# Rotary embedding on one core: VectorE and GpSimd start at slot 120 of 128

## The chip, the core and the metric

The kernel runs on one core of a Trainium2 chip. A core has several engines with an instruction list of its own each: TensorE (PE in the profile) for matrix products, VectorE (DVE) and GpSimd (POOL) for elementwise work, ScalarE (ACT) for functions and copies, SyncE (SP), which here only issues transfers. Sixteen DMA engines move data between the main memory (HBM) and the on-chip memory; a transfer is issued by an instruction of SP or of ACT and joins that engine's queue. Engines wait for one another and for transfers by semaphores. The metric is the device time of one execution in microseconds (us); less is better.

## The reference

For x of shape (8, 2048, 8, 64) and tables cos and sin of shape (2048, 32), all float32:

```python
x1 = x[..., : x.shape[-1] // 2]
x2 = x[..., x.shape[-1] // 2 :]
out1 = x1 * cos - x2 * sin     # cos, sin broadcast over batch and head
out2 = x1 * sin + x2 * cos
return np.concatenate([out1, out2], axis=-1)
```

So each element is read once, multiplied by a cosine, and gets its partner from the other half times a sine added. x and the result have 33.55 MB each.

## The kernel before

**Tiling.** The 2048 positions of one batch are laid over the 128 partitions, 16 to each; a batch is then one tile `xt` of 128x8192 float32 (4 MB). There are five such buffers (NBUF = 5). Batches 0 to 4 are loaded at the start, and the load of batch b + 5 is issued behind the work on batch b; it needs the buffer, and so waits until the store of batch b is done. Loads go to SP's queue; stores of batches 0 to 6 go to ACT's queue, those of the last batch to SP's. The result overwrites `xt` before it is stored. Batch 0 is loaded in three parts and stored in two, batch 7 is stored in three.

**Work on a batch.** `rotate` treats a piece of 128x2048 (the two halves of a quarter in batches 0 and 7 are 128x1024). A piece has one of three kinds:

- kind A (29 pieces): POOL makes `t2`, the partner times the sine, in two products (line 122); DVE makes `t1`, x times the cosine (line 129), and adds the two into `xt` (line 136);
- kind B (the first piece of batches 2, 4 and 5): the same two products, but TensorE adds them by multiplying with a unit matrix `eye` (lines 143 and 144), and ACT copies the sum back (line 145);
- kind C (the first piece of batches 1 and 3): DVE makes both products (lines 129 and 148), TensorE adds them with `eye` or its negative `neye` (lines 160 and 161), and ACT copies the sum back (line 165).

**The start.** ACT issues the load of sin (line 76), SP those of the first quarter of batch 0, of cos, and of the rest (lines 67 and 69). POOL writes `eye` by a memset and a select (lines 80 and 81). When sin has landed, ACT writes `nsin`, `sin_ps` and `neye` (lines 90 to 92). When cos has landed, DVE copies it to `cos_ps` (line 93). Then the loop over batches begins.

**Order.** Nearly every instruction stands in `keep(...)`, which holds it at its place in the written order; the order of an engine's instructions is that of the program text. What an engine does first on the page is its part of a barrier of all engines (line 208 in the profile), and last its part of a closing barrier (line 219). Beside the instructions of the program text the lists hold small ones: where an instruction waits for more semaphores than fit into it, an EVENT_SEMAPHORE instruction ahead of it waits for the rest.

Of the kernel before, what the change touches and what calls it, by code (L numbers as in the profile page):

```python
# [10 lines left out]
def kernel(  # L11
# [7 lines left out]
    nc = tc.nc  # L19
    keep = tc.keep_in_program_order  # L20
# [30 lines left out]
    eye = const_pool.tile([P, P], f32, tag="eye")  # L51
# [25 lines left out]
    for b in range(NBUF):  # L77
        load(b)

    nc.gpsimd.memset(eye, 0.0)  # L80
    nc.gpsimd.affine_select(
        out=eye,
        in_=eye,
# [140 lines left out]
```

## Time and profile before

| | |
|---|---|
| time, median of 3 runs | 163.61 us (163.48 to 163.63) |
| span of the profiled execution | 161.8 us, 459 instructions |
| around the span (median less span) | 1.8 us |
| DVE busy | 140.1 us (87%), 66 instructions |
| POOL busy | 138.9 us (86%), 70 instructions |
| PE busy | 49.4 us, ACT 12.8 us |
| moved by DMA | 67.65 MB, 418 GB/s over the span |

The profile is of one execution; its own time is given only as the span, from the first to the last of the program's instructions. The median is that of other, timed runs; it is 1.8 us above the span, for what lies ahead of and behind the program. Busy time is the time in which an engine worked; waits, branches and the issue of transfers are not in it. A share of the whole span says little of a single stage: DVE, for one, stands still for the first 6.93 us and is nearly always busy from there to the last add.

The queues in the DMA part of the page are q1 (SP's), q10 (ACT's) and one called "instruction", over which the engines' instruction lists are brought in.

### The profile page before, as it was taken

Reading aid. Unit: us, or ns where it says so; the run is one execution under the profiler, and the core shown is the slowest. Engines: PE = TensorE matmul, PEld = TensorE weight load, DVE = VectorE, ACT = ScalarE, POOL = GpSimd, SP = SyncE. Lnnn points to the kernel's source line nnn. Section 1 sums busy time; section 2 is a strip of 40 time slices with the busy share of each in tenths; the row PEclk is TensorE's granted clock in tenths of the full one; section 3 lists DMA queues with packets and bytes.
Section 4 is the critical chain, followed back from the end, with each engine's and each line's share of the span. In section 5 each row is a group of like instructions: output and inputs, shape, how many; then the busy total and the mean of one; then the engine's idle time right before and its main releaser. Section 6 shows DMA issues by size and latency. Waiting matters only on the chain.

```text
span 161.8 us, 459 instructions
## 1 busy us (share of the span) xinstructions
PE 49.4 (31%) x80; PEld 18.5 (11%) x80; DVE 140.1 (87%) x66; ACT 12.8 (8%) x14; POOL 138.9 (86%) x70
## 2 busy tenths in 40 slices
PE   0000000597309760978049714972000000000000
PEld 0000000142004220322023301330000000000000
DVE  0297999999999999999999999199989999899950
ACT  3300000002200220021000220022000000000000
POOL 1399997998999999992999959999899997999800
PEclk9999999999975998589957995699655555555555
DMA  5999999999999999899899999999999999999995
GB/s 158 425 454 494 413 308 446 413 470 405 462 405 462 389 502 405 389 510 397 389 510 397 389 512 397 397 502 397 397 488 413 405 478 413 405 478 409 397 419 225
DMA packets 3314, 67.65 MB, mean 418 GB/s; under 512 B 368, under 2 KB 368, under 8 KB 624
## 3 DMA queue, kind: packets, MB, share of 16 engines
q1 hardware_dynamic: 2016, 38.01, 55.5%
q10 hardware_dynamic: 1296, 29.62, 42.6%
q14 instruction: 2, 0.02, 0.0%
HBM read 34.08 MB, written 33.55 MB: 418 GB/s over the span
## 4 chain that ended last, share of the span: by engine, by line
DMA 48%; DVE 37%; POOL 9%; issue 2%; DVEq 0%; SPq 0%; POOLq 0%; ACTq 0%
DMA xt<-in_x_dram 26%; DVE t L129 18%; DMA out_dram<-xt 18%; DVE xt L136 17%; POOL t L122 9%; DMA sin_sb<-in_sin_dram 4%; DVE t L148 1%; DVEq L136 0%; SPq L67 0%; POOLq L122 0%; ACTq L74 0%
## 5 line engine op out<-in xcount | busy, mean ns | idle before, releaser
L122 POOL TENSOR_TENSOR t<-xt,sin_sb 128x1024 f32<-128x1024 f32 (+1 forms) x32 | 70.4, 2199 | 13.5 <-DMA xt<-in_x_dram 8.3
L129 DVE TENSOR_TENSOR t<-xt,cos_ps 128x2048 f32<-128x2048 f32 (+1 forms) x34 | 73.4, 2167 | 0.8
L122 POOL TENSOR_TENSOR t<-xt,nsin 128x1024 f32<-128x1024 f32 (+1 forms) x32 | 70.3, 2196 | 0.0
L136 DVE TENSOR_TENSOR xt<-t,t 128x2048 f32<-128x2048 f32 (+1 forms) x29 | 62.2, 2145 | 8.2 <-POOL t L122 5.5
L143 PE MATMUL o<-t,eye 128*128 128x512 f32 x24 | 17.0, 799 | 23.1 <-DVE t L129 19.6
L160 PE MATMUL o<-t,eye 128*128 128x512 f32 x16 | 12.0, 844 | 37.8 <-DVE t L129 35.6
L144 PE MATMUL o<-t,eye 128*128 128x512 f32 x24 | 14.9, 709 | 0.0
L145 ACT COPY xt<-o 128x1024 f32<-128x1024 f32 x6 | 6.1, 1012 | 45.7 <-PE o L144 45.7
L143 PEld LDWEIGHTS o<-t,eye 128*128 128x128 f32 x24 | 5.5, 256 | 32.5 <-issue 26.5
L160 PEld LDWEIGHTS o<-t,eye 128*128 128x128 f32 x16 | 3.7, 256 | 43.2 <-issue 39.4
L165 ACT COPY xt<-o 128x1024 f32<-128x1024 f32 x4 | 4.0, 1012 | 47.8 <-PE o L161 47.8
L93 DVE COPY cos_ps<-cos_sb 128x512 f32<-128x512 f32 x1 | 0.7, 695 | 6.9 <-DMA cos_sb<-in_cos_dram 6.9
L144 PEld LDWEIGHTS o<-t,eye 128*128 128x128 f32 x24 | 5.6, 234 | 8.2 <-issue 7.6
L161 PE MATMUL o<-t,neye 128*128 128x512 f32 x8 | 6.3, 875 | 0.2
L148 DVE TENSOR_TENSOR t<-xt,sin_ps 128x2048 f32<-128x2048 f32 x2 | 4.6, 2281 | 0.0
L161 PE MATMUL o<-t,eye 128*128 128x512 f32 x8 | 4.1, 592 | 0.0
L161 PEld LDWEIGHTS o<-t,neye 128*128 128x128 f32 x8 | 2.2, 300 | 5.3 <-issue 3.6
L161 PEld LDWEIGHTS o<-t,eye 128*128 128x128 f32 x8 | 1.5, 190 | 1.9 <-issue 1.9
L90 ACT ACT_TABLE_LOAD x1 | 1.3, 1283 | 1.2 <-PEq L208 1.2
L90 ACT ACTIVATE nsin<-sin_sb 128x512 f32<-128x512 f32 x1 | 0.6, 629 | 4.0 <-DMA sin_sb<-in_sin_dram 4.0
L91 ACT COPY sin_ps<-sin_sb 128x512 f32<-128x512 f32 x1 | 0.6, 580 | 0.0
L80 POOL MEMSET eye<- 128x128 f32 x1 | 0.2, 204 | 0.3 <-POOLq L208 0.3
(6 smaller groups left out, 1.0 us busy)
## 6 DMA issues: line engine op xcount, KB each, us to landing
xt<-in_x_dram SPq DMA_DIRECT2D x7, 4096.0 KB, 42.8
out_dram<-xt ACTq DMA_DIRECT2D x6, 4096.0 KB, 27.2
out_dram<-xt ACTq DMA_DIRECT2D x2, 2048.0 KB, 22.3
xt<-in_x_dram SPq DMA_DIRECT2D x2, 1024.0 KB, 6.7
xt<-in_x_dram SPq DMA_DIRECT2D x1, 2048.0 KB, 12.2
out_dram<-xt SPq DMA_DIRECT2D x1, 2048.0 KB, 9.9
out_dram<-xt SPq DMA_DIRECT2D x2, 1024.0 KB, 6.2
sin_sb<-in_sin_dram ACTq DMA_DIRECT2D x1, 256.0 KB, 5.7
```

Of the source, the lines that this page charges most:

```text
L90: keep(nc.scalar.mul(nsin, sin_sb, -1.0))
L93: keep(nc.vector.tensor_copy(cos_ps, cos_sb))
L122: nc.gpsimd.tensor_mul(out=t2u[:, :, u, :].rearrange("p (r h) d -> p r h d", h=H), in0=xu[:, :, 1 - u, :].rearrange("p (r h) d -> p r h d" ...
L129: nc.vector.tensor_mul(out=t1.rearrange("p (r k d) -> p r k d", r=nr, d=Dh), in0=xk, in1=rep(cos_ps[:, r0 : r0 + nr, :], 2 * H),)
L136: keep(nc.vector.tensor_add(out=xt, in0=t1, in1=t2))
L143: nc.tensor.matmul(oc, eye, t1[:, cs], start=True, stop=False)
L144: nc.tensor.matmul(oc, eye, t2[:, cs], start=False, stop=True)
L145: keep(nc.scalar.copy(xt[:, 2 * j * C : 2 * (j + 1) * C], o))
L148: nc.vector.tensor_mul(out=t2.rearrange("p (r k d) -> p r k d", r=nr, d=Dh), in0=xk, in1=rep(sin_ps[:, r0 : r0 + nr, :], 2 * H),)
L160: nc.tensor.matmul(oc, eye, t1u[:, gs, u, :], start=True, stop=False)
L161: nc.tensor.matmul(oc, eye if u else neye, t2u[:, gs, 1 - u, :], start=False, stop=True)
L165: nc.scalar.copy(xu[:, :, u, :], o.rearrange("p (g d) -> p g d", d=Dh))
```

## The change

Two directives are put ahead of POOL's first instruction of the program text and ahead of DVE's, and the memset behind them is held in its place:

```diff
-    nc.gpsimd.memset(eye, 0.0)
+    for eng in (nc.vector, nc.gpsimd):
+        keep(eng.addr_align(128, offset=120))
+    keep(nc.gpsimd.memset(eye, 0.0))
     nc.gpsimd.affine_select(
```

`addr_align(128, offset=120)` is not an instruction that the engine runs. When the program is loaded it is dropped, and empty instructions are put in its place, as many as it takes for the instruction behind it to stand 120 slots past a multiple of 128 in that engine's list (a slot is the place of one instruction). That can be none and at most 127, and the engine runs through all of them. On DVE the instruction behind it is the copy to `cos_ps`, on POOL the first one of writing `eye`. Both directives stand behind the opening barrier. No other instruction is added, taken out or moved on any engine; line numbers behind the change grow by two.

## The prediction
> **What bounds the kernel now.** I began with the page's slices of the span.
>
> ```profile
> DVE  0297999999999999999999999199989999899950
> POOL 1399997998999999992999959999899997999800
> DMA  5999999999999999899899999999999999999995
> DMA packets 3314, 67.65 MB, mean 418 GB/s; under 512 B 368, under 2 KB 368, under 8 KB 624
> ```
>
> Each digit is 4.05 us. The DMA engines are full from the second slice to the last but one; DVE and POOL are nearly full too, but each has its empty part at the left edge. What ended the empty parts is in the waits of the two engines, of which I read POOL's and then DVE's:
>
> ```profile
> POOL t L122 <- DMA xt<-in_x_dram: 8.3, 6, 3.0
> POOL t L122 <- DMA sin_sb<-in_sin_dram: 5.2, 1, 5.2
> ...
> DVE cos_ps L93 <- DMA cos_sb<-in_cos_dram: 6.9, 1, 6.9
> DVE xt L136 <- POOL t L122: 5.5, 4, 3.6
> ```
>
> (total us, times, longest). At the start both wait for tables. Later POOL waits six times for a batch to land, 8.3 us in all, and DVE four times for POOL. The timeline of the first 8 us puts places to this:
>
> ```profile
> 0.73 0.20 POOL L80 MEMSET eye<- 128x128 f32 x1 [0.29 <-POOLq L208]
> ...
> 1.01 0.29 POOL L81 TENSOR_SCALAR_AFFINE_SELECT eye<-eye 128x128 f32<-128x128 f32 x1
> ...
> 6.53 1.26 POOL L122 TENSOR_TENSOR t<-xt,sin_sb 128x512 f32<-128x512 f32 x1 [5.23 <-DMA sin_sb<-in_sin_dram]
> 6.93 0.69 DVE L93 COPY cos_ps<-cos_sb 128x512 f32<-128x512 f32 x1 [6.93 <-DMA cos_sb<-in_cos_dram]
> ...
> 7.53 0.30 ACT L92 ACTIVATE neye<-eye 128x128 f32<-128x128 f32 x1
> ```
>
> The chain that ended last, in order of time, holds these two pieces:
>
> ```profile
> 62.55 28.82 DMA out_dram<-xt
> ...
> 91.50 42.82 DMA xt<-in_x_dram
> ```
>
> The store of batch 2 frees a buffer, the load of batch 7 takes it, lands at 134.3, and the last 21.6 us of compute and the last store follow. But the load waited in its queue: batch 6, ahead of it, landed only at 114.9 (POOL's wait for it ends there), 23 us after batch 7's load was issued. Both queues together were moving all that the DMA engines could. So the bound is the DMA, with a tail of compute behind the last load; DVE and POOL come close behind.
>
> **The change, part by part.** *The empty instructions, their number.* The program's lists show one directive on each of the two engines, no count. It depends on the slot at which each list stood before, which no view shows. The page has two packets on the instruction queue within the span,
>
> ```profile
> q14 instruction: 2, 0.02, 0.0%
> ```
>
> and the trace's packet records put them at 94.4 and 120.0 us, 8192 bytes and 309 ns each. I read each as an engine that enters a new block of its list and has a further block brought in, and 8192 bytes as 128 slots (64 bytes each). At 94.4 DVE's sequencer stood at its 65th entry (waits counted), at 120.0 POOL's stood at about its 70th to 74th. If the packets are theirs, a block ended there, DVE's copy (third entry) stood at slot 66 and POOL's memset at some 62 to 66, and the padding is 54 to 58 on both. That the two agree speaks for it; but TensorE and ScalarE were also moving near 94, so I keep 0 and 127 as ends and take 55.
>
> *Price of one.* No row has an empty instruction. The nearest are entries that the sequencer deals with alone: two MODIFY_POOL_CONFIG of POOL start 30 ns apart (0.88 and 0.91), two semaphore waits of POOL 78 ns (0.53 and 0.61), two of DVE 69 ns (119.24 and 119.31), all met at once. So 30 to 78 ns on POOL and 30 to 69 ns on DVE; as the semaphore entries do more than an empty one, I take 50 ns. That makes 55 x 0.05 = 2.75 us on each (the ends: 0, and 127 x 0.078 = 9.9 us on POOL, 127 x 0.069 = 8.8 us on DVE).
>
> [...]
>
> *What covers it.* POOL is done with the opening barrier at 0.73, needs 0.57 us for `eye` (0.73 to 1.30), and has nothing to do until the first quarter of batch 0 (6.30) and sin (6.46) are there: 6.30 - 0.73 - 0.57 = 5.0 us of cover. DVE waits from 0.69 to 6.93: 6.2 us. With 2.75 us both are covered, cost 0. `eye` is ready at 1.30 + 2.75 = 4.05; ScalarE takes it at 7.53, TensorE at 30.1: cost 0. SP and ACT issue all the first loads by themselves and wait for neither engine: cost 0. If the cover is gone, POOL is late by up to 9.9 - 5.0 = 4.9 us and DVE by up to 8.8 - 6.2 = 2.6. The delay runs on into the chain, and the stores of batches 0 to 2 are late by as much. It would not reach the end, though: POOL waits for the landings of batches 1, 2 and 4 for 0.9, 0.7 and 3.0 us and for batch 5's for 1.7, which swallows 6.3 us by 96 us; while stores are missing, the loads have the DMA engines to themselves and land rather sooner; and the load of batch 7 has 23 us in its queue. From 134.45 on nothing is left to swallow a delay.
>
> *The block's end, moved.* With the first instruction at slot 120 a block ends 8 slots on: on DVE behind the add at 11.63, on POOL at about 10 us. Before, DVE's adds and products around 94.4 follow each other at the usual 2.40 us (92.47 to 94.86), POOL's around 120.0 at 2.28 (119.59 to 121.86): entering a block cost nothing measurable. I take 0 here as well; the packet itself is 0.3 us of one of 16 engines. The upper end, if the block were not there in time: what a fresh transfer needs in that crowd, 6.7 us for a 1 MB load of batch 0. It would fall on both engines at once, at a place from where the later waits swallow most.
>
> [...]
>
> *`keep` on the memset.* The lists show the same order as before: 0.
>
> **Sum.** 161.8 us of span + 0 + 0 + 0, and 1.8 us around it: 163.6, the median of the runs (163.61).
>
> **Rivals.**
> *Slower, a long padding* (0.12). Padding near 127 at near 78 ns, from the point where it passes 5.0 us on POOL. Against it: 54 to 58 by the packets, and the waits that swallow. If the early delay is paid in full in the chain (store of batch 2, load of batch 7), it costs up to 4.9; with half of that, 163.6 + 2.4 = 166.0.
> *Slower, a block's end in a bad place* (0.18). DVE's 111 entries from the copy on now end at slot 231, before at 177; the next block's end, at 256, is 25 slots into what follows instead of 79. If the closing part is longer than 25 and the block isn't there, or if the block at 10 us isn't, the stall decides. For it: the closing part lies behind everything and hides nothing. Against it: blocks were there in time twice before. Price: 0.3 us (a packet) to 6.7; near the low end, since a block has over 140 us to come: 163.6 + 1.0 = 164.6.
> *Faster, later stores* (0.16). If the padding is visible by 1 to 3 us, loads land sooner for want of stores beside them, and the waits for batches 1 to 7 shrink. The last, 1.14 us at 134.45 for batch 7, is the gain if it goes whole: 162.5. The DMA share of the last 5.8 us is only 0.67, so there is room. Against it: with 55 x 0.05 nothing is visible. A share of it comes at 0.4 to 0.6 us.
> *Nothing happens* (padding of few or no instructions) ends at 163.6 like the forecast and is in its chance.
>
> **Numbers.** The measurement tells about 0.2% from no change, 0.33 us. Forecast, hidden padding (or none): 0.54, within 0.2%. Faster 0.16, slower 0.12 + 0.18 = 0.30. The likeliest case alone has 163.3 to 163.9. For 8 in 10 I leave out the better half of the faster case (0.08) and most of the long padding (0.10), which gives 163.0 to 165.2.
>
> **What would show it.** Right: DVE's copy still starts at about 6.93, POOL's first product at 6.53, `eye` at 2 to 5 us instead of 0.73, and batch 7's product still at 134.45. The two packets of the instruction queue move to about 10 to 13 us. Wrong: POOL's first product later than 6.6 (padding not covered); a gap of over 0.2 us in DVE or POOL between 9 and 13 us with no semaphore behind it (block not there); the span unchanged but the time not (closing part); a shorter or longer wait for batch 7.

## The result, and the profile after

The changed kernel takes 164.29 us (median of 5 runs, 163.99 to 164.47) against 163.60 us (163.48 to 163.63): ratio 1.0037, 95% interval 1.0026 to 1.0048. A second comparison of the same two kernels gave 163.98 against 163.59 us, ratio 1.0020 (1.0011 to 1.0029). The change costs 0.2 to 0.4%. Both times lie inside the stated range; the first is clear of the forecast "within 0.2%", the second at its edge. The span of the profiled execution grew from 161.8 to 162.5 us. Every ratio here leaves out slow executions, those over 1.5% above the fastest of their kernel: five of the eleven of `branch_8` and one each of `wait_only` and `copy_1`.

The start went as forecast. From the timeline of the changed kernel (start, us, engine, line, operation, tiles; line numbers are two higher):

```profile
2.81 0.20 POOL L82 MEMSET eye<- 128x128 f32 x1 [2.37 <-issue]
3.09 0.29 POOL L83 TENSOR_SCALAR_AFFINE_SELECT eye<-eye 128x128 f32<-128x128 f32 x1
...
6.53 1.26 POOL L124 TENSOR_TENSOR t<-xt,sin_sb 128x512 f32<-128x512 f32 x1 [3.15 <-DMA sin_sb<-in_sin_dram]
6.93 0.69 DVE L95 COPY cos_ps<-cos_sb 128x512 f32<-128x512 f32 x1 [6.93 <-DMA cos_sb<-in_cos_dram]
```

The trace records 53 empty instructions on DVE (they start from 0.76 to 3.19 us, 47 ns apart) and 52 on POOL (0.69 to 2.73, 40 ns apart). They moved `eye` by 2.08 us and nothing else: the first products start at 6.53 and 6.93 as before, and every row of both engines stays within 0.02 us of its place until 22.8 us. Then the load of batch 1 is late. The timeline around it, before:

```profile
22.78 2.33 POOL L122 TENSOR_TENSOR t<-xt,nsin 128x1024 f32<-128x1024 f32 x1
...
26.04 2.33 POOL L122 TENSOR_TENSOR t<-xt,sin_sb 128x1024 f32<-128x1024 f32 x1 [0.93 <-DMA xt<-in_x_dram]
```

and after:

```profile
22.80 2.31 POOL L124 TENSOR_TENSOR t<-xt,nsin 128x1024 f32<-128x1024 f32 x1
...
27.63 2.33 POOL L124 TENSOR_TENSOR t<-xt,sin_sb 128x1024 f32<-128x1024 f32 x1 [2.51 <-DMA xt<-in_x_dram]
```

POOL is done at the same time and waits 1.6 us longer. It stays so. The waits of POOL after (total us, times, longest):

```profile
POOL t L124 <- DMA xt<-in_x_dram: 9.9, 6, 3.5
```

and those of DVE:

```profile
DVE xt L138 <- POOL t L124: 7.4, 6, 3.2
```

Both grew, from 8.3 and 5.5. Batch 7's first product on POOL, in the timeline of before:

```profile
134.45 2.33 POOL L122 TENSOR_TENSOR t<-xt,sin_sb 128x1024 f32<-128x1024 f32 x1 [1.14 <-DMA xt<-in_x_dram]
```

and of after:

```profile
136.14 2.33 POOL L124 TENSOR_TENSOR t<-xt,sin_sb 128x1024 f32<-128x1024 f32 x1 [1.20 <-DMA xt<-in_x_dram]
```

It starts 1.69 us late. The last add, in the timeline of before and of after:

```profile
154.79 1.23 DVE L136 TENSOR_TENSOR xt<-t,t 128x1024 f32<-128x1024 f32 x1
```

```profile
156.49 1.23 DVE L138 TENSOR_TENSOR xt<-t,t 128x1024 f32<-128x1024 f32 x1
```

It ends 1.69 us late (157.71 instead of 156.02). The end moved by 0.67 only. The last store landed 4.86 us after its issue before (156.05 to 160.91), and 3.84 us after it now (157.74 to 161.58). The piece of the result ahead of it landed 2.44 us after that issue before (158.49) and 1.31 us after it now (159.05), so the last store had less in front of it, and 1.0 us came back.

Why the landing was late is in the trace's packet records and in the 16 landings of each transfer, read here as one for each of the 16 DMA engines (16 packets are under way at once for 145.8 of the 161.8 us before). The packet behind another is the one that starts within 12 ns of its end (of two such at 15.99 us, the long one). All times in us, packets in ns:

```
packets on the instruction queue, and the packet behind each
before   94.39  309 ns, behind it a 32 KB packet of 1564 ns
        120.00  309 ns, behind it a 32 KB packet of 1429 ns
after     9.89  309 ns, behind it a 16 KB packet of  932 ns
         15.99  319 ns, behind it a 32 KB packet of 1875 ns
usual: 16 KB 611 ns, 32 KB 1213 ns

landings        median   third last   second last   last
batch 1 before   25.71      25.88        25.89      25.90
batch 1 after    25.57      25.93        26.39      27.50
batch 7 before  133.51     134.00       134.25     134.32
batch 7 after   133.30     133.69       134.30     136.01
```

Fourteen of the 16 landings of batch 1 are where they were. One is 0.5 us behind them and one 1.6. The tile waits for the last one: it is at 27.50, and POOL's product starts at 27.63 (before, 25.90 and 26.04). The packet of the block that is brought in takes 309 ns (319 in one row), and the packet behind it takes 0.2 to 0.7 us more than usual: 932 - 611 = 321 and 1875 - 1213 = 662 after, 351 and 216 before. That sums to 0.63 and 0.98 us of one engine each. The records do not name the engine. Followed from packet to packet, an engine has several continuations within 10 ns at some steps, so that the late landings are those of the engines with the two blocks is argued here and not shown. The 0.98 us also falls short of the 1.6 us by which the last landing is behind; the rest has no explanation in this trace. In the runs below with one block fetched early, loss and lag do agree. The DMA engines have no gap to speak of (a mean busy share of 0.97 to 1.04 in every stage from 1.5 to 148 us), and a last landing that is behind at batch 1 is followed by others: for batches 1 to 7 it lies 1.56, 1.55, 2.16, 2.14, 2.17, 2.18 and 2.32 us behind the third last, against 0.03 to 0.78 before. That it is the same engine each time is argued and not shown.

### The profile page after: what moved, and what is told of

It reads as the page before. It is cut to its first block, busy times and chain, and to the rows that moved or that the text cites. A ratio compares the mean times of both kernels' runs of the same rounds, so it can differ in the third digit from the quotient of the medians.

```text
span 162.5 us, 564 instructions
## 1 busy us (share of the span) xinstructions
PE 47.8 (29%) x80; PEld 18.0 (11%) x80; DVE 140.1 (86%) x66; ACT 12.8 (8%) x14; POOL 139.0 (86%) x70
## 4 chain that ended last, share of the span: by engine, by line
DMA 51%; DVE 27%; POOL 9%; PE 4%; issue 4%; SPq 1%; ACT 1%; DVEq 0%; POOLq 0%; ACTq 0%
DMA xt<-in_x_dram 51%; DVE t L131 14%; DVE xt L138 12%; POOL t L124 9%; PE o L145 2%; PE o L146 2%; DVE t L150 1%; SPq L67 1%; ACT xt L147 1%; SPq L69 0%; DVEq L138 0%; POOLq L124 0%; ACTq L147 0%
## 5 line engine op out<-in xcount | busy, mean ns | idle before, releaser
L145 PE MATMUL o<-t,eye 128*128 128x512 f32 x24 | 17.3, 813 | 25.1 <-DVE t L131 21.7
L162 PE MATMUL o<-t,eye 128*128 128x512 f32 x16 | 10.7, 756 | 39.1 <-DVE t L131 36.9
L146 PE MATMUL o<-t,eye 128*128 128x512 f32 x24 | 14.8, 702 | 0.0
L163 PE MATMUL o<-t,neye 128*128 128x512 f32 x8 | 5.8, 818 | 0.2 <-DVE t L150 0.2
L163 PE MATMUL o<-t,eye 128*128 128x512 f32 x8 | 4.1, 592 | 0.0
```

What stands on the lines that cost most here:

```text
L145: nc.tensor.matmul(oc, eye, t1[:, cs], start=True, stop=False)
L146: nc.tensor.matmul(oc, eye, t2[:, cs], start=False, stop=True)
L162: nc.tensor.matmul(oc, eye, t1u[:, gs, u, :], start=True, stop=False)
L163: nc.tensor.matmul(oc, eye if u else neye, t2u[:, gs, 1 - u, :], start=False, stop=True)
```

## The experiments

Theory F: the fetched blocks, brought in early, put DMA engines behind. Its rivals are P, that the empty instructions cost by themselves; C, that the late landing is chance; and others named where they came up. Each ratio is to the kernel before, on the same chip in the same rounds, with its 95% interval.

**One engine's alignment alone**

```diff
-    for eng in (nc.vector, nc.gpsimd):
+    for eng in (nc.vector,):         # dve_only
+    for eng in (nc.gpsimd,):         # pool_only
```

> VectorE alone gets the alignment, GpSimd's list is that of before. Theory F (each instruction block that is fetched holds up one of the 16 DMA engines; brought in early, it makes every later landing late): of the two early packets on the instruction queue one is left (VectorE's, by the order of its entries the one at 16.0 us), the other goes back to 120.0. The load of batch 1 lands at about 27.5 us instead of 25.9, that of batch 7 1.5 to 1.7 us late, and the time is 164.1 to 164.3. Theory C (the landing of batch 1 is late by chance of the packets' interleaving and has nothing to do with the fetch): no packet predicts a lag; landings like before or anything else, 163.6 +- 0.5. Theory P (the empty instructions themselves cost): half of the loss, 163.9.

> GpSimd alone gets the alignment. Theory F: the packet at 9.9 us stays, the other goes back to 94.4. The packet at 9.9 held its DMA engine for 309 ns and the next one for 321 ns longer than usual, so one of the 16 landings of batch 1 is 0.5 to 0.6 us later than the rest (26.4), and batch 7 lands up to 0.5 us late: 163.6 to 163.9, less than half of the loss. Theory C: nothing predictable. Theory P: 163.9.

DVE alone: 164.06 us, 1.0028 (1.0018 to 1.0038). Its packet is at 15.94, with a packet of 1861 ns behind it (309 + 648 ns lost), and the other is back at 120.97; batch 1 lands at 25.81 (third last) and 26.69 (last). POOL alone: 163.80 us, 1.0011 (1.0002 to 1.0020); packets at 10.07 (934 ns behind it, 309 + 323 lost) and 94.20, last landing at 26.67 against 25.89. So the packet at 94 was DVE's and that at 120 POOL's, as the prediction read them. DVE's block carries most of the loss, and the two add up to 0.39%, next to the 0.37% of the first comparison of both. The lag in DVE's run is 0.9 us, not the 1.6 forecast, and batch 7 landed 0.1 us later than before (134.44), not 1.5 to 1.7; but that is a profile of 163.80 us, the fastest of this kernel's eight executions.

**The same from an engine that computes nothing here at that time**

```diff
+    keep(nc.scalar.addr_align(128, offset=124))
     keep(nc.scalar.mul(nsin, sin_sb, -1.0))
```

> VectorE's and GpSimd's lists are those of before; ScalarE is aligned to slot 124 behind the issue of sin's load, so that its block ends after four entries, near 7 us, while it waits for sin anyway. Theory F: a third packet on the instruction queue at about 9 to 12 us beside the two at 94.4 and 120.0, one landing of batch 1 later than the other 15 by 0.5 to 1.6 us, 163.8 to 164.3, although no engine that computes starts differently. Theory P and every theory that needs VectorE's or GpSimd's list: 163.6.

163.72 us, 1.0010 (1.0001 to 1.0019). A third packet came at 7.21, and one landing of batch 1 (26.57) is 0.6 us behind the rest (25.98), though DVE and POOL had their old lists. The lag follows the packet (309 + 316 ns lost) and not the two engines' lists. Its price is small: below what was expected, and close to none.

**Empty time without a block's end**

```diff
+    busy = t1s_pool.tile([P, UNIT], f32, tag="t1s")
+    keep(nc.vector.memset(busy, 0.0))
+    busy2 = t1s_pool.tile([P, UNIT], f32, tag="t1s")
+    keep(nc.gpsimd.memset(busy2, 0.0))
-    nc.gpsimd.memset(eye, 0.0)
+    keep(nc.gpsimd.memset(eye, 0.0))
```

> No alignment. VectorE and GpSimd each begin with one memset of a scratch tile of 128x2048, about 2 us of work that nothing reads, in the place of the 53 and 52 empty instructions; the lists shift by one entry. Theory F: the two instruction packets stay near 94 and 120, landings like before, 163.6 (163.5 to 163.8). Theory P (an engine that starts its work some 2 us later costs the time, by the late eye or otherwise): 164.1 to 164.3.

From the timeline of this run, DVE's memset (POOL's starts at 0.73 and takes 1.80 us):

```profile
1.23 1.76 DVE L81 MEMSET busy<- 128x2048 f32 x1 [1.23 <-PEq L212]
```

The engines were occupied for nearly as long as by the empty instructions, and the packets stayed at 94.3 and 120.8. 163.78 us, 1.0008 (0.9999 to 1.0017): P has at most 0.17%. It is also as much as POOL's block alone (1.0011) and ScalarE's (1.0010) came out at, so that those two cost anything by their packets is not shown; DVE's 1.0028 is well above it. In the profiled execution one landing of batch 1 was 0.5 us behind the rest all the same (26.78 against 26.25), with no block fetched early. So landings fall behind in other ways too, and a single landing does not prove a cause; the medians have to.

**The changed kernel again, and a later end of the block**

```diff
-        keep(eng.addr_align(128, offset=120))
+        keep(eng.addr_align(128, offset=90))     # mid_90, both engines
```

> The changed kernel once more, beside the next three. Theory F (each block of instructions that is fetched holds up one of the 16 DMA engines; early, the lag stays to the end): packets on the instruction queue at about 9.9 and 16.0 us again, the last landing of batch 1 1.0 us or more behind the second to last, of batch 7 1 to 2.3 us behind the third to last, 164.1 to 164.4. If the late landing were chance (theory C), the last landing would be back at the others.

> Both engines aligned to slot 90 instead of 120: 30 empty instructions fewer on each, and the block ends 38 entries on instead of 8. Theory F: the two packets come at about 55 to 70 us; batches 1 to 3 land as before, one landing of batches 4 or 5 on is late by 0.6 to 2, batch 7 lands late by about 0.5 to 1.7, and the time is between 163.6 and 164.3. Theory P: the loss shrinks with the padding, by 30/53: 163.9. Theory C: landings of batch 1 anywhere.

> Slot 90 on both engines once more, on another chip if it falls so: packets at about 60 us. Theory E: between the run of before and the changed kernel, 163.7 to 163.9. Theory H: 163.6 to 163.8, since stores share the engines at 60 us.

The second run of the changed kernel is the one told above (1.0020). Its packets were at 10.39 and 15.84 and cost nearly as much as in the first (309 + 318 and 309 + 628 ns), but in the profiled execution (163.86 us, below its own median) the last landing of batch 1 was only 0.2 us behind (26.36 against 26.17), against the 1.0 or more expected. Batch 7 landed no later than before (134.27), POOL waited 7.8 us for landings instead of 8.3, and the last add ended at 155.95; yet the last store landed at 161.18, 0.27 us later than before, 0.5 us behind the third last of its 16 landings. So of the two profiles of the changed kernel only the first shows the path by way of late loads and late compute; in the second the loss lies in the last store. The lag varies from run to run, and so do the times: 163.6 to 164.5. With the block's end 38 entries on, both packets come at 60.3 to 60.6 us: 163.71 us, 1.0008 (0.9999 to 1.0017), and again 163.69 us, 1.0003 (0.9994 to 1.0012). No loss that can be told, and batch 7 landed at 133.97 and 134.00, not late as expected. The packets behind these blocks were held up by 271 to 571 ns.

**Early, or early among loads alone?** After the first runs there were two explanations: that an early lag lasts longer (E), or that it matters where in the stream of transfers it falls (H). H took the size of the hold-up for the reason. The edit is shown against the changed kernel:

```diff
-    for eng in (nc.vector, nc.gpsimd):
-        keep(eng.addr_align(128, offset=120))
+    for eng in (nc.vector,):
+        keep(eng.addr_align(128, offset=112))    # dve_112; offset=124: dve_124
```

> VectorE alone, at slot 112 instead of 120: its block ends 16 entries on, and the packet should come at 20 to 25 us, when stores share the DMA engines (the first is issued at 18.4 us), instead of 16.0, when loads have them alone. Theory H (what an early packet costs is the hold-up of the packet behind it on its DMA engine, 628 to 662 ns at 16 us against 216 ns at 120 us for the same engine's block, because in the stage of loads alone there is no other queue to fill the gap): hold-up 200 to 550 ns, 163.6 to 163.85. Theory E (being early is what costs, since the lag lasts to the end): like the run with VectorE alone at slot 120, 163.9 to 164.2.

163.61 us, 0.9997 (0.9989 to 1.0006). The packet moved from 15.9 to 25.3 us and the loss was gone. No landing of batch 2 was behind (40.49, 40.51, 40.52), though the hold-up was 1747 - 1213 = 534 ns, nearly that at 16 us. E falls: over 136 us were still to come. H's place is right, but its reason is not, since the hold-up hardly shrank. (From 18 to 30 us, while the stores begin, other packets are long too, up to 2087 ns in the kernel before, so this one hold-up is less certain than those elsewhere; the blocks at 60 us say the same.) Theory L keeps the place and gives another reason: where loads run alone all engines are level, and the one that is held up is the last from then on.

> VectorE alone, at slot 124: its block ends after four entries, near 9 us, packet at 11 to 14 us, inside the stage of loads alone but on another transfer than at 16.0. Theory L: as at slot 120, a landing of batch 1 0.5 to 0.9 us behind the rest and 163.8 to 164.2. If the place at 16.0 us alone matters: 163.6 to 163.7.

> Both engines at slot 112 instead of 120, that is eight empty instructions fewer and the block's end 16 entries on: both packets at 20 to 27 us, behind the first store's issue (18.4 us). Theory L (a packet on one DMA engine costs where loads alone run, because all 16 engines are level there and the one that is held up is last from then on; with stores between, the engines are up to 1.1 us apart and a held-up one is hidden): 163.6 to 163.7, no landing of batch 2 behind the rest. Theory E (early costs): 163.9 to 164.3.

DVE at slot 124: packet at 13.61 us, behind it 1867 ns (325 + 654 lost), one landing of batch 1 at 26.95 with the third last at 26.04, 164.05 us, 1.0023 (1.0012 to 1.0035). So another place among the loads costs like that at 16 us. Both engines at slot 112: 163.69 us, 1.0000 (0.9992 to 1.0009); packets at 18.34 and 25.52, the first of them when the first store was being issued (18.4). This is the changed kernel with eight empty instructions fewer on each engine, and the whole loss is gone. The timeline shows batch 1 on POOL:

```profile
27.01 2.34 POOL L124 TENSOR_TENSOR t<-xt,sin_sb 128x1024 f32<-128x1024 f32 x1 [1.83 <-DMA xt<-in_x_dram]
```

Here the landing of batch 1 was 1.0 us later than before, and that of batch 2 was behind too, against the expectation (41.20 last, 40.70 third last); yet the time did not move. By batch 7 the last landing is at 134.38, where it is at 134.32 before. In the kernel before, whose blocks are fetched at 94 and 120, a landing is behind late in the run anyway: the last of batch 5 is at 95.75 with the third last at 94.97. That a block is the cause is not shown. It may be that a lag of 0.6 to 0.7 us taken early takes the place of one taken late; no run tries that by itself.

**Plain packets in place of fetched blocks.** DVE's and POOL's lists are those of before; ScalarE, done with `neye` at 7.83 us before, issues small transfers that nothing reads, each from one row of x into one partition of a scratch tile: four of 2047 float32 (8188 bytes) in `copy_4`, four of 2048 (8192 bytes) in `copy_4_even`, which was meant to spread each over the DMA engines.

```diff
+    scrap = t1s_pool.tile([P, UNIT], f32, tag="t1s")
+    for k in range(4):
+        keep(nc.scalar.dma_start(out=scrap[k : k + 1, 0:2047], in_=xv[0, k : k + 1, 0:2047]))
     keep(nc.vector.tensor_copy(cos_ps, cos_sb))
# copy_4_even: 0:2048;  copy_1: one transfer
# copy_4_spread: out=scrap[16 * k : 16 * k + 16, 0:128], in_=xv[0, 16 * k : 16 * k + 16, 0:128]
# copy_4_late: the same four behind rotate of batch 1's first piece
```

> The lists of VectorE and GpSimd are those of before. [...] Theory F: no matter what is in the packet, if the four go to one engine it falls behind by 4 x 0.3 us or more, one landing of batch 1 is 1.2 to 2.5 us behind the others, and the time is 164.0 to 164.6; if they go to four engines, four landings lag by 0.3 to 0.6 and the time is 163.6 to 163.9. Theory I (it is particular to an instruction's fetch): 163.6.

> [...] Theory F: no landing falls behind, 163.6 to 163.7. If the extra issues or their semaphores cost time by themselves, this run shows it as well.

> As the runs with four extra transfers of 8 KB, which went as one packet each (that of 2048 elements too); now each of the four is 16 rows of 512 bytes, so that the same bytes, issues and waits are there but every DMA engine gets a sixteenth. Theory F or H: no landing falls behind the rest, 163.6 to 163.8, against 164.5 for the single packets. If 164.3 or more comes out, the extra issues, or the loads that they make SP issue later (batch 2 at 9.9 instead of 3.2 us), cost the time, and the runs with the single packets say nothing of DMA engines.

> One plain single packet of 8188 bytes instead of four, at 10 to 12 us. Theory L: 0.3 us or more on one DMA engine in the stage of loads alone, a landing of batch 1 0.3 to 0.6 us behind the rest, 163.65 to 163.95; the cost grows with the number of packets (four: 164.5). If a single landing behind the rest has no price: 163.6.

> The four plain single packets of 8188 bytes once more, but issued by ScalarE behind its copies for batch 1 (at about 42 us), in the stage in which stores and loads share the DMA engines; they stand behind a store in ACT's queue and move at about 50 us. Theory L: at most 1.1 us of the 1.2 or more that they take is hidden, 163.6 to 164.0, less than half of the 0.9 us that they cost at 10 to 15 us. If the stage does not matter: 164.3 to 164.7.

Four packets of 8188 bytes: 164.53 us, 1.0051 (1.0039 to 1.0063), as expected for one engine. They moved at 10.46, 11.98, 13.51 and 14.43, 309 ns each, at distances that one or two 16 KB packets of the loads fill, as on one engine; the packets behind them took the usual 611 and 1213 ns and were not held up. That is 4 x 0.309 = 1.24 us of one engine. Batch 1's last landing, at 26.92, was 1.0 us later than before, but only 0.4 us behind the third last, not the 1.2 to 2.5 expected; batch 7's (135.03) was 0.7 us later than before. The run meant as control (2048 elements) failed as one: its transfers were not spread but single packets of 8192 bytes too, at 10.57 to 14.55, and it repeats the finding, 164.47 us, 1.0046 (1.0032 to 1.0060). The control that held is the one over 16 rows: the same bytes and the same four issues, now in 64 packets of 512 bytes, 163.75 us, 1.0003 (0.9994 to 1.0011). One thing differs: SP issued the load of batch 4 at 14.31 us in it and at 26.94 in the run with four packets (9.41 before). Batches 2 and 3 stand ahead of that load in the queue, and batch 3 landed only at 56 us before, so the later issue leaves no gap. From its timeline, batch 1 on POOL:

```profile
26.04 2.33 POOL L125 TENSOR_TENSOR t<-xt,sin_sb 128x1024 f32<-128x1024 f32 x1 [1.04 <-DMA xt<-in_x_dram]
```

As four single packets 32 KB cost 0.9 us; as 64 packets they cost nothing that can be told. One packet alone: 163.68 us, 0.9999 (0.9990 to 1.0008), against the expected 163.65 to 163.95 at its low end; 0.31 us of one engine costs nothing that can be told. Four packets late (they moved at 53.2 to 60.2 us): 164.14 us, 1.0040 (1.0013 to 1.0068). That is above the expected 163.6 to 164.0 and below the 164.3 of the other side. In that run the last add ended early, at 155.38, and the last store landed late, at 161.33: probably the engine with the four packets was itself the last to finish, which the records, without the engine's name, do not show. Three of that kernel's loads were also issued later (batch 4's at 38.3 instead of 9.4, batch 6's at 81.4 instead of 72.1 and batch 7's at 100.9 instead of 91.5), so it is no clean measure of the stage.

**No empty instruction to run**

```diff
-        keep(eng.addr_align(128, offset=120))
+        keep(eng.addr_align(128, offset=8, max_nops=0))
```

> Both engines at slot 8 with no empty instruction to run (a branch leaps the padding), so that each enters a new block right behind the opening barrier and then has all of its 111 or fewer entries in it. Two packets on the instruction queue at 2 to 4 us, when the first loads (8 KB packets) have just begun, and none at 94 and 120. Theory H: the packet behind is short, the hold-up small, the engines catch up while the queues fill: 163.3 to 163.7. Theory E: the lag is there from the start, 163.9 to 164.4.

Neither expectation held: 1.0074 (1.0040 to 1.0108), the highest ratio of all the edits. The only profile is of an execution of 169.04 us, while the ratio rests on those of 164.12 to 166.33. In it the packets came at 1.79 and 3.65, the first of 944 ns, among the transfers of the tables, and POOL's first product started late:

```profile
7.22 1.27 POOL L124 TENSOR_TENSOR t<-xt,sin_sb 128x512 f32<-128x512 f32 x1 [5.50 <-DMA sin_sb<-in_sin_dram]
```

That is 7.22 instead of 6.53. But with no block fetched that early the same product started at 6.89 in `wait_only`, at 6.90 in `after_again` and at 7.03 in `copy_4`, so the row does not show that the packets delayed the tables. What costs 0.7% here stays open. No version beat the kernel before.

**The lag, run by run.** How far the last landing of a batch lies behind the third last, from the 16 landings in each profile, with the end of the last add and the last landing of all (us):

```
                   batch 1   batch 7   last add ends   last landing
before               0.03      0.32       156.02          160.91
changed kernel       1.56      2.32       157.71          161.58
  again              0.28      0.42       155.95          161.18
DVE, slot 120        0.88      0.88       156.14          161.13
DVE, slot 124        0.90      0.90       156.40          161.39
DVE, slot 112        0.05      0.10       155.50          160.90
both, slot 112       0.68      0.16       156.08          161.04
16 rows              0.10      0.57       156.02          160.91
```

For DVE alone at slots 120 and 124 the block and its hold-up took 0.96 and 0.98 us of one engine, and one landing lies 0.9 us behind at batch 1 and as far at batch 7. There the last add is 0.1 to 0.4 us late and the last landing 0.2 to 0.5.

## Why the prediction was wrong

*The empty instructions, their number and price: right.* 53 and 52 against 55, just below its 54 to 58; 47 and 40 ns against 50; 2.5 and 2.1 us against 2.75, all of it under the cover. The reading of the two packets as 128 slots each, from which the count came, is borne out. `eye` at 2.81 lay in the forecast's 2 to 5.

*What the cover hides: right.* But for `eye`, not one row of either engine moved before the load of batch 1 landed.

*The block's end, moved: this step failed.* It had the packets go "to about 10 to 13 us". They went to 9.9 and 16.0: DVE reaches the ninth entry from the aligned one at 12.1, and its packet moves 3.9 us later. It was right that the engines that enter the block lose nothing: no gap on DVE or POOL there. It then priced the packet as "0.3 us of one of 16 engines" and took 0. That treats the delay as if all 16 shared it: the tile waited for the last of the 16 landings (27.50 us, with POOL's product at 27.63), and in the two runs with DVE's block alone, at slots 120 and 124, the last landing, 0.9 us behind at batch 1, was as far behind at batch 7. And the packet's price was half missing: 309 ns, and a further 321 and 662 ns on the packet behind it. The term that was set to 0 measured 0.2 to 0.4% (0.4 to 0.7 us).

*The later waits swallow a delay: wrong in the first profile.* They could swallow late compute; there the landings themselves were late, and POOL's wait for them grew from 8.3 to 9.9 us instead of shrinking. At the end 1.0 of 1.7 us came back, by a tail that the prediction did not count as cover. In the second profile of the changed kernel the waits did end on time, and 0.27 us were lost in the landing of the last store, behind which there is no wait to swallow anything.

*Rivals.* The long padding did not come about. The rival with the block's end in a bad place had the right object and the wrong victim: it let an engine wait for its instructions, and what was late was the landing of a load (27.50 instead of 25.90 us). Its price (0.3 us for a packet, taken as 1.0) lies near the measured 0.4 to 0.7 by luck, since it stood for a stall of a compute engine. The faster rival needed a visible padding, which there was not.

*What stays open.* The runs show that 0.9 us or more of a single engine costs where loads run alone (1.0023 and 1.0028 for one block of DVE, 1.0046 and 1.0051 for four plain packets), that 0.3 costs nothing there that can be told, that 0.6 costs 0.1% or nothing, and that DVE's block at 25 us, both blocks at 18 and 25 us and both at 60 us cost nothing that can be told. So the place of the packets is shown to matter, and so is whether the same bytes come as four packets or as 64. Why the place matters is not: theory L forecast slot 124 and the single packet rightly, for both engines at slot 112 it had the time right and the landings wrong, and four packets late cost more than it allowed. That the lag of 0.7 us in the run with both at slot 112 is free because it replaces a late one of the kernel before is argued from the landings of batch 7 and not tried. Why the engine with the block at 25.3 us, with 0.84 us lost, was not behind at all is open as well; the 16 landings of batch 1 lie 0.4 to 1.2 us apart in the profiles without an early lag, so it may have been one of the early ones, but the records do not name the engine.

## What to carry to other kernels

When the DMA engines are full (a share of 0.97 to 1.04 here), ask of every small transfer, one of instructions too, whether it goes as a single packet: the work here waited for the last of a load's 16 landings, and in three of the profiles that landing, 0.9 to 1.6 us behind the third last at batch 1, was 0.9 to 2.3 us behind it at batch 7, 108 us later. Spread small transfers over 16 rows (1.0003 here, against 1.0051 for the same bytes as single packets). Moving a block's end by eight entries was worth 0.2 to 0.4% here, so small changes at a program's start can move the time without touching its work.

## What the runs showed of the hardware

- An instruction block came as one packet of 8192 bytes (at 94.39 and 120.00 us before, at 9.89 and 15.99 in the changed kernel). That it holds 128 entries fits every slot tried: DVE's packet moved at 13.6, 15.8 to 16.0, 25.3 to 25.5 and about 60 us with the first entry at slots 124, 120, 112 and 90 of 128.
- The packet behind a fetched block was longer than usual: by 318 to 323 ns for a 16 KB packet (`after_again`, the changed kernel, `pool_only`), by 216 ns (before, at 120.00 us) to 662 ns (the changed kernel, at 15.99) for a 32 KB packet. In the kernel before, the only 32 KB packets over 1245 ns from 30 us on are the two behind blocks. Behind a plain packet of 8188 bytes in `copy_4` it was not (611 and 1213 ns, the usual).
- A transfer of 2048 float32 in one partition went as one packet of 8192 bytes, not in 16 parts (`copy_4_even`, four packets at 10.57 to 14.55 us), one of 2047 as one of 8188 (`copy_4`: eight packets more than before in all, four of them under 512 B). Over 16 rows each, the same four transfers went as 64 packets of 512 bytes, with 64 under 512 B beside them (`copy_4_spread`).
- Empty instructions started 47 ns apart on VectorE (53 of them) and 40 ns apart on GpSimd (52) in the changed kernel.
- In the kernel before, packets of loads (1213 ns for 32 KB) and of stores (1213 ns, 611 for 16 KB) mostly alternate once stores run: of the 1097 packets of 4 KB or more between 22 and 120 us behind which exactly one such packet starts within 4 ns of their end, 963 are followed by one of the other queue.
